# Three issue orders pinned in a two-layer encoder kernel: copies, a weight and two sums

## The chip, the cores and the metric

The kernel runs on one core of a Trainium2 chip. The metric is the time of one execution on the device in microseconds. A core has five engines that each work through their own list of instructions and wait for each other by semaphores: TensorE (PE in the profile: matmuls), ScalarE (ACT), VectorE (DVE), GpSimd (POOL) and SyncE (SP). The last two here mostly issue transfers.

## What is computed

Two layers over 512 tokens of 1024 channels, all in fp32, and a last normalisation:

```python
for l in range(DEPTH):                      # DEPTH = 2
    x = x + 0.5 * swiglu(rms_norm(x, ffn1_norm[l]), ffn1_w_in[l], ffn1_w_out[l])
    x = x + mixer(rms_norm(x, mix_norm[l]), mix_w_in[l], mix_gate_bias[l], na_rpb[l],
                  na_w_out[l], f_w_out[l], mix_w_o[l])
    x = x + 0.5 * swiglu(rms_norm(x, ffn2_norm[l]), ffn2_w_in[l], ffn2_w_out[l])
return rms_norm(x, final_norm)
```

The feed-forward width is 2816. The mixer projects its normalised input to queries, keys, values, Fourier input and two gates, and ends with

```python
y_na = neighbourhood_attention(q, k, v, rpb) @ w_na_out
y_f = fourier_mix(uf) @ w_f_out
g_na = jax.nn.sigmoid(ga + gate_bias[0])
g_f = jax.nn.sigmoid(gf + gate_bias[1])
return (g_na * y_na + g_f * y_f) @ w_o
```

## The kernel before

**Precision.** Every operand of a matmul is split in two parts of a shorter format, high (`hi`, written by ScalarE as a copy) and low (`lo`, what is left, written by VectorE). A product is then three matmuls, high by high, high by low and low by high. Lines 490, 491 and 493 of `late_low` issue them, with the ones that need the weight's low part last in their group.

**Strassen's products.** Most of the large products are done as seven products of half the size, numbered 1 to 7, instead of eight. Their operands are sums and differences of quarters of the activations and of the weights. The activations' sums are made by VectorE and split (`combo`, `parts`; names t1, t2, ... or m1, m2, ...). One half-size product takes two items of weights (two granules), and writes two banks of the accumulation memory (`pair("A")`, `"B"`, `"C"`; `"wA"`, `"wB"`, `"wC"` in the output product). A is used again: products 6, 7 and 4 add into the banks that product 1 began.

**The stream of weights.** `Stream` holds all weight items in order. `next()` gives the item that a product needs now, and first calls `prep`, which prepares the items up to two ahead: it asks for the transfers of items up to eight further (`fetch`, issued on SP's queue at line 147, the added second part on POOL's at line 149), makes a sum of two transferred weights where the item is one (L163), writes the high part `whi` (L190, or L185 with a sign) and the low part `wlo` (L193, or L186). For `whi` and `wlo` there are three buffers each, so an item's high part waits until TensorE is done with the item three before. In the gates and the output product, product 6's raw weight gets a further part added by a transfer on POOL's queue once product 6 is prepared (L195), and is then product 3's.

**Order.** Instructions are traced in program order. A scheduler, which runs at build time with a model of the machine, then chooses each engine's order: among the instructions that it takes to be ready, the one traced first. Two means pin it. Instructions traced in a block `tc.manual_schedule(engines=...)` keep their order on those engines. In a block `tc.issue_after(ins)`, whatever is traced on the engine of `ins` is issued behind `ins`; nothing waits for `ins` to end.

**The plain block** is the first work of the first layer (`stage_ffn`, `if first`). The 256 columns of gate and 256 of up that are left over are computed as a plain product of eight steps over the channels, from four weight items (`ws.items[0]` to `[3]`), into the banks `cl`. In the same place, in a block with pinned order for VectorE and ScalarE, the differences of the activations are made that Strassen's products need (L660, L661, L665, L667, and their parts).

**The gates** (`gate_block`, called twice in each layer's mixer) do the seven products in the order 1, 5, 2, 6, 7, 3, 4. After product 6, `snap(pa)` copies both banks of A with ScalarE (L560), and the gate's tanh follows (L1348); product 7 then adds into the same banks. In the first block of each layer `fourth` follows, which makes the operand of product 4.

**The output product** at the end of the mixer (`stage_mixer`, from L1700) does the same on the gated sum, which is first turned to channels by transposes (L1424, copied out in L1425; `mq`). Products 1, 5 and 2 run first; the operands of product 6 (a6) and product 2 (a2) are made while TensorE does product 1 and 5.

Of the kernel before, what the change touches and what calls it, by code (L numbers as in the profile page):

```python
# [13 lines left out]
AF = mybir.ActivationFunctionType  # L14
ALU = mybir.AluOpType
# [74 lines left out]
def encoder_kernel(  # L90
# [3 lines left out]
    V, S, G, PE = nc.vector, nc.scalar, nc.gpsimd, nc.tensor  # L94
# [15 lines left out]
    def slot(dt=F32, s="k", shape=(4, 256)):  # L110
        return kp.tile([P, *shape], dt, tag="k", name=nm(s), bufs=23)
# [8 lines left out]
    def pair(s="ps"):  # L120
        return [bank(s), bank(s)]
# [188 lines left out]
    ws = Stream()  # L310
# [7 lines left out]
    def split(hi, lo, src, scale=None):  # L318
        if scale is None:
            S.activation(hi, src, AF.Copy)  # L320
            V.tensor_tensor(lo, src, hi.bitcast(F32), ALU.subtract)
            return
        S.activation(hi, src, AF.Copy, scale=scale)
        V.scalar_tensor_tensor(lo, src, scale, hi.bitcast(F32), ALU.mult, ALU.subtract)
# [161 lines left out]
    def late_low(parts, again=False):  # L486


        for ps, lh, ll, rh, _, start, _ in parts:
            PE.matmul(ps, lh, rh, start=start, stop=False, skip_group_check=again)  # L490
            PE.matmul(ps, ll, rh, start=False, stop=False, skip_group_check=again)  # L491
        for ps, lh, _, _, rl, _, stop in parts:
            PE.matmul(ps, lh, rl, start=False, stop=stop, skip_group_check=again)  # L493

    def product(ps, acts, kts, start, stop=True, again=False, hook=None, by_block=False, ahead=AHEAD):

        h, l, off = acts
        n = (len(kts) + 1) // 2  # L500

        def granule(i, w, b):
            res = []
            for k, kt in enumerate(kts[2 * i : 2 * i + 2]):
                c, z = slice(off + b * P, off + (b + 1) * P), slice(k * T, (k + 1) * T)
                res.append((
                    ps[b], h[:, kt, c], l[:, kt, c], w[0][:, z], w[1][:, z], start and i + k == 0,
                    stop and 2 * i + k == len(kts) - 1,
                ))
            return res  # L510

        if by_block:
            w = [ws.next() for _ in range(n)]
            for b in range(2):
                for i in range(n):
                    late_low(granule(i, w[i], b), again)
            return
        for i in range(n):
            w = ws.next(AHEAD if i < n - 1 and ahead else ahead)
            if i < n - 1:  # L520
                late_low(granule(i, w, 0) + granule(i, w, 1), again)
            else:
                late_low(granule(i, w, 0), again)
                late_low(granule(i, w, 1), again)
            if hook and i == 0:
                hook()
# [19 lines left out]
    def combo(dst, in0, in1, op, s):  # L546
        V.tensor_tensor(dst, in0, in1, op)
        return parts(dst, s)

    def parts(src, s):  # L550
        h, l = slot(F32R, s + "h"), slot(F32R, s + "l")
        split(h, l, src)
        return h, l, 0
# [3 lines left out]
    def snap(ps):  # L557
        t = slot(F32, "sn", (2, T))
        for b in range(2):
            S.activation(t[:, b, :], ps[b], AF.Copy)  # L560
        return t

    def less(ps, t):
        for b in range(2):
            res = V.tensor_tensor(t[:, b, :], ps[b], t[:, b, :], ALU.subtract)  # L565
        return res
# [30 lines left out]
    def stage_ffn(norm, nxt, late):  # L597
# [50 lines left out]
        if first:  # L648
            for g in range(2):
                w = ws.next()  # L650
                for kk in range(2):
                    plain(2 * g + kk, w, kk, (0, 1))
            w2 = [ws.next(), ws.next()]
            for js in ((1,), (0,)):
                for g in range(2):
                    for kk in range(2):
                        plain(4 + 2 * g + kk, w2[g], kk, js)
            with tc.manual_schedule(engines={mybir.EngineType.DVE, mybir.EngineType.Activation}):
                b11, b12, b21, b22 = raw[0, 0], raw[0, 1], raw[1, 0], raw[1, 1]
                V.tensor_tensor(b11, b11, b12, ALU.subtract)  # L660
                V.tensor_tensor(b12, b12, b22, ALU.subtract)  # L661
                acts[5] = parts(b11, "t1")
                norm.squares(0, 0)
                norm.squares(1, 0)
                V.tensor_tensor(b22, b22, b11, ALU.add)  # L665
                acts[7] = parts(b12, "t3")
                V.tensor_tensor(b21, b21, b22, ALU.subtract)  # L667
                acts[6] = parts(b22, "t2")
                ws.prep(ws.pos + 3)
                norm.squares(0, 1)  # L670
                norm.squares(1, 1)
                split(*t4, b21)
# [162 lines left out]
        for jb in range(0 if first else 1, NB):  # L835
            f0 = 2 + 4 * jb
            if first and jb == 0:
                with tc.manual_schedule(engines={mybir.EngineType.DVE, mybir.EngineType.Activation}):
                    pa = pair("A")
                    product(pa, acts[1], K4, True)  # L840
                    for j in range(2):
                        t = snap(pcl[j])
# [33 lines left out]
        ps = {}  # L876
# [120 lines left out]
    def stage_mixer(l, norm, nxt):  # L997
# [338 lines left out]
        def gate_block(i, bias, acts, after):  # L1336

            r = norm.r

            def arg(src, which, j):  # L1340
                t = src if src is not None else slot(F32, "ga", (2, T))
                for b in range(2):
                    c = 2 * j + b
                    V.scalar_tensor_tensor(
                        t[:, b, :], pa[b] if src is None else t[:, b, :], r[:, c : c + 1],
                        bias[which][:, i * T : (i + 1) * T], ALU.mult, ALU.add,
                    )
                S.activation(t, t, AF.Tanh, scale=0.5)  # L1348
                return t

            def gated(t, y):
                V.scalar_tensor_tensor(y, t, 1.0, y, ALU.add, ALU.mult)

            done = []

            def both(j):

                if j in done and (i, j) in ns:
                    V.tensor_tensor(fs[i, j], fs[i, j], ns[i, j], ALU.add)
                done.append(j)  # L1360

            def with_f(t, j):
                gated(t, fs[i, j])
                both(j)

            def with_n(t, j):
                if (i, j) in ns:
                    gated(t, ns[i, j])
                    both(j)
                else:  # L1370
                    ga[j] = t

            ga = [None, None]
            for m in ORDER:
                if m == 1:
                    pa = pair("A")
                    product(pa, acts[1], K4, True)
                    s1 = snap(pa)
                elif m == 5:
                    pb = pair("B")  # L1380
                    product(pb, acts[5], K4, True)
                    sb = snap(pb)
                elif m == 6:
                    product(pa, acts[6], K4, False, again=True)
                    with tc.manual_schedule(engines={mybir.EngineType.Activation}):
                        s2 = snap(pa)
                        with_n(arg(s1, 0, 0), 0)
                elif m == 2:
                    pc = pair("C")
                    product(pc, acts[2], K4, True)  # L1390
                    less(pc, s1)
                elif m == 7:
                    product(pa, acts[7], K4, False, again=True)
                    less(pa, sb)
                    with_f(arg(sb, 1, 1), 1)
                elif m == 3:
                    product(pb, acts[3], K4, False, again=True)
                    less(pb, s2)
                    with_n(arg(s2, 0, 1), 1)
                else:  # L1400
                    product(pa, acts[4], K4, False, again=True)
                    with_f(arg(None, 1, 0), 0)
                if m in after:
                    after[m]()
            return ga if (i, 0) not in ns else [fs[i, 0], fs[i, 1]]
# [46 lines left out]
        with tc.manual_schedule(engines={mybir.EngineType.DVE, mybir.EngineType.Activation}):  # L1452
            with tc.manual_schedule(engines={mybir.EngineType.PE}):
# [60 lines left out]
                for s in range(3):  # L1514
                    t = slot(F32R, "vs", (2, T))
# [184 lines left out]
        def fourth():  # L1700
            with behind_weights():
                V.tensor_tensor(t12, B[1, 0][0], t12, ALU.subtract)
                V.tensor_tensor(t12, t12, B[1, 0][1], ALU.add)
                split(hx[0][:, :, 256:512], lx[0][:, :, 256:512], t12)

        ga0 = gate_block(0, bias, acts, {1: third_parts, 6: fourth})

        ga1 = gate_block(1, bias, acts, {5: lambda: to_channels(0, ga0, 1), 2: lambda: to_channels(0, ga0, 0)})
        m00, m01 = mq[0, 0], mq[0, 1]
        a1 = parts(m00, "m1")  # L1710
# [7 lines left out]
        m11 = mq[1, 1]  # L1718
        to_channels(1, ga1, 0)
        m10 = mq[1, 0]  # L1720
        a6 = combo(m00, m00, m11, ALU.add, "m6")
        a2 = parts(m10, "m2")
        pb = pair("wB")
        product(pb, a5, K4, True)
        put(pb, 1, 1, -1)
# [220 lines left out]
```

## Time and profile before

| | us |
|---|---|
| three runs: lowest, median, highest | 1896.66, 1898.59, 1898.66 |
| the profiled execution, as timed | 1897.87 |
| its span, first to last instruction | 1896.1 |
| TensorE busy in it | 1883.8 |
| VectorE busy | 1647.4 |
| ScalarE busy | 1188.6 |
| GpSimd busy | 171.5 |

A row of the order of time has the start in us from the span's start, the time that the instruction (or a run of equal ones, x their number) took, the engine, the line of the kernel, the operation, what it writes `<-` what it reads, their shapes, and in brackets how long the engine had been idle before and what ended that. A row of the list of waits has who waited `<-` for whom, the time in all, how many times, and the longest. In a row of stretches, the busy time of TensorE, its weight loads, VectorE, ScalarE and GpSimd stands with the number of instructions, and then the granted clock, the share of the transfer engines and GB/s.

### The profile page before, as it was taken

How to read it: one execution, taken by the hardware profiler on the slowest of the kernel's cores; microseconds unless marked ns; L12 is line 12 of the kernel's file. 1: busy time of each engine (PE TensorE's matmuls, PEld its weight loads, DVE VectorE, ACT ScalarE, POOL GpSimd, SP SyncE). 2: the span in 40 equal slices, each digit the busy share in tenths (PEclk: the TensorE clock that was granted, in tenths of full speed). 3: DMA queues.
4: the chain of work that ended last, by engine and by line, in shares of the span. 5: the costliest groups of instructions: out<-in, count | busy, mean ns of one | idle time of the engine just before them, and what ended most of it. 6: DMA issues, size and time to landing. Idle time of an engine off the chain costs nothing.

```text
span 1896.1 us, 25080 instructions
## 1 busy us (share of the span) xinstructions
PE 1883.8 (99%) x9150; PEld 1578.6 (83%) x9150; DVE 1647.4 (87%) x2006; ACT 1188.6 (63%) x1700; POOL 171.5 (9%) x210
## 2 busy tenths in 40 slices
PE   9999999999999999999999999999999999999998
PEld 7888888888888888888888888888888888888886
DVE  7877899788989987889998778998889899887899
ACT  6655665668665755566665556666685576556664
POOL 0101011100111010001010100101001101100010
PEclk9999999999999999999999999999999999999999
DMA  9777498932886777649867764988248867766594
GB/s 302 208 201 189 152 244 262 230 102 98 242 219 163 183 191 204 178 151 258 254 193 202 194 174 154 267 267 213 84 137 229 215 169 177 207 177 178 173 278 143
DMA packets 106940, 372.75 MB, mean 197 GB/s; under 512 B 12288, under 2 KB 12416, under 8 KB 106816
## 3 DMA queue, kind: packets, MB, share of 16 engines
q1 hardware_dynamic: 78144, 272.80, 41.7%
q0 software_dynamic: 28528, 98.33, 28.5%
q8 instruction: 72, 1.18, 0.2%
q14 instruction: 52, 0.43, 0.1%
q10 hardware_dynamic: 144, 0.02, 0.0%
HBM read 365.85 MB, written 2.11 MB: 194 GB/s over the span
## 4 chain that ended last, share of the span: by engine, by line
PE 96%; DMA 1%; DVE 1%; issue 1%; SPq 0%; ACT 0%; POOL 0%; DVEq 0%; POOLq 0%; ACTq 0%
PE A L490 10%; PE A L491 10%; PE A L493 10%; PE o L493 7%; PE o L490 7%; PE o L491 7%; PE B L490 5%; PE B L491 5%; PE B L493 5%; PE ps L314 4%; PE ps L315 4%; PE ps L316 3%; PE C L491 2%; PE C L490 2%; PE C L493 2%; PE tr L613 2%
## 5 line engine op out<-in xcount | busy, mean ns | idle before, releaser
L190 ACT ACTIVATE whi<-raw 128x1024 fp32r<-128x1024 f32 (+1 forms) x534 | 551.4, 1037 | 388.5 <-PE A L491 124.2
L193 DVE TENSOR_TENSOR wlo<-raw,whi 128x1024 fp32r<-128x1024 f32 (+1 forms) x534 | 633.3, 1192 | 167.7 <-ACT whi L190 166.4
L149 POOL DMA_DIRECT2D raw<-in_wst_dram x166 | 144.4, 899 | 1369.9 <-DMA raw<-in_wst_dram 927.9
L163 DVE TENSOR_TENSOR raw<-raw,raw 128x1024 f32<-128x1024 f32 (+1 forms) x150 | 177.4, 1190 | 1.2
L490 PE MATMUL A<-whi,xh 128*128 128x512 f32 x400 | 155.7, 389 | 0.0
L491 PE MATMUL A<-whi,xl 128*128 128x512 f32 x400 | 155.7, 389 | 0.0
L493 PE MATMUL A<-wlo,xh 128*128 128x512 f32 x400 | 115.1, 389 | 0.0
L185 ACT ACTIVATE whi<-raw 128x1024 fp32r<-128x1024 f32 (+1 forms) x83 | 85.8, 1037 | 42.2 <-PE o L491 14.0
L186 DVE SCALAR_TENSOR_TENSOR wlo<-raw,whi 128x1024 fp32r<-128x1024 f32 (+1 forms) x83 | 98.0, 1194 | 12.7 <-ACT whi L185 12.7
L695 ACT ACTIVATE th<-sn,rh 128x512 f32<-128x512 f32 x80 | 56.9, 715 | 69.7 <-DVE sn L565 69.7
L560 ACT ACTIVATE sn<-A 128x512 f32<-128x512 f32 x104 | 60.8, 589 | 45.8 <-PE A L493 45.7
L493 PEld LDWEIGHTS A<-wlo,xh 128*128 128x128 f32 x400 | 75.1, 188 | 15.6
L491 PEld LDWEIGHTS A<-whi,xl 128*128 128x128 f32 x400 | 75.1, 188 | 15.4
L490 PEld LDWEIGHTS A<-whi,xh 128*128 128x128 f32 x400 | 75.1, 188 | 15.4
L490 PE MATMUL C<-whi,xh 128*128 128x512 f32 x208 | 81.2, 390 | 0.0
L491 PE MATMUL C<-whi,xl 128*128 128x512 f32 x208 | 81.0, 389 | 0.0
L490 PE MATMUL B<-whi,xh 128*128 128x512 f32 x208 | 81.0, 389 | 0.0
L491 PE MATMUL B<-whi,xl 128*128 128x512 f32 x208 | 81.0, 389 | 0.0
L493 PE MATMUL C<-wlo,xh 128*128 128x512 f32 x208 | 59.8, 389 | 0.0
L493 PE MATMUL B<-wlo,xh 128*128 128x512 f32 x208 | 59.8, 389 | 0.0
L490 PE MATMUL B<-whi,t5h 128*128 128x512 f32 x136 | 54.3, 399 | 0.0
L715 DVE TENSOR_TENSOR at<-at,at 128x1024 f32<-128x1024 f32 (+1 forms) x48 | 53.7, 1127 | 0.0
(448 smaller groups left out, 4786.0 us busy)
## 6 DMA issues: line engine op xcount, KB each, us to landing
raw<-in_wst_dram SPq DMA_DIRECT2D x470, 512.0 KB, 5.4
raw<-in_wst_dram POOLq DMA_DIRECT2D x174, 512.0 KB, 8.1
raw<-in_wst_dram SPq DMA_DIRECT2D x30, 256.0 KB, 4.1
bm<-in_bias_dram SPq DMA_DIRECT2D x16, 384.0 KB, 3.8
vs<-v SPq DMA_DIRECT2D x12, 256.0 KB, 3.8
x<-in_xin_dram SPq DMA_DIRECT2D x4, 512.0 KB, 10.2
raw<-in_wst_dram POOLq DMA_DIRECT2D x8, 256.0 KB, 8.2
dft<-in_dft_dram POOLq DMA_DIRECT2D x8, 256.0 KB, 4.4
```

What stands on the lines that cost most here:

```text
L149: G.dma_start(out=self.t, in_=wst[GRAN_AT[self.plus]][:, 0 : self.n], accum_op=ALU.add)
L163: V.tensor_tensor(self.raw.t, self.raw.t, self.add.t, ALU.add)
L185: S.activation(hi, t, AF.Copy, scale=-1.0)
L186: self.last = V.scalar_tensor_tensor(lo, t, -1.0, hi.bitcast(F32), ALU.mult, ALU.subtract)
L190: S.activation(hi[:, cs], t[:, cs], AF.Copy)
L193: self.last = V.tensor_tensor(lo[:, cs], t[:, cs], hi[:, cs].bitcast(F32), ALU.subtract)
L314: PE.matmul(ps, lh, rh, start=start, stop=False, skip_group_check=again)
L315: PE.matmul(ps, lh, rl, start=False, stop=False, skip_group_check=again)
L490: PE.matmul(ps, lh, rh, start=start, stop=False, skip_group_check=again)
L491: PE.matmul(ps, ll, rh, start=False, stop=False, skip_group_check=again)
L493: PE.matmul(ps, lh, rl, start=False, stop=stop, skip_group_check=again)
L560: S.activation(t[:, b, :], ps[b], AF.Copy)
```

## The change

Three places get an issue order. No instruction is added or taken out.

1. *Plain block.* What VectorE does in the block of differences is issued behind the low part of the fourth weight item, the plain block's last.
2. *Gates.* `snap` keeps its last copy's instruction. Before product 7, the fetch that the coming preparation would ask for is asked for, and the preparation up to product 3's first weight is traced in a block behind the second copy of product 6: on ScalarE, `whi` of that weight is issued after both copies.
3. *Output product.* The sum for product 6 with its parts, the parts for product 2, and the preparation of weights up to product 2's first are put in one block with pinned order for VectorE and ScalarE.

```diff
@@ snap
-            S.activation(t[:, b, :], ps[b], AF.Copy)
+            snapped[0] = S.activation(t[:, b, :], ps[b], AF.Copy)
         return t
+
+    snapped = [None]
@@ stage_ffn, plain block
-            with tc.manual_schedule(engines={mybir.EngineType.DVE, mybir.EngineType.Activation}):
+            with (
+                tc.issue_after(ws.items[3].last.ins),
+                tc.manual_schedule(engines={mybir.EngineType.DVE, mybir.EngineType.Activation}),
+            ):
                 b11, b12, b21, b22 = raw[0, 0], raw[0, 1], raw[1, 0], raw[1, 1]
                 V.tensor_tensor(b11, b11, b12, ALU.subtract)
@@ gate_block
                     with tc.manual_schedule(engines={mybir.EngineType.Activation}):
                         s2 = snap(pa)
+                        copied = snapped[0]
                         with_n(arg(s1, 0, 0), 0)
...
                 elif m == 7:
+                    ws.fetch(ws.pos + 2 + ws.depth)
+                    with tc.issue_after(copied.ins):
+                        ws.prep(ws.pos + 3)
                     product(pa, acts[7], K4, False, again=True)
@@ stage_mixer, output product
-        a6 = combo(m00, m00, m11, ALU.add, "m6")
-        a2 = parts(m10, "m2")
+        with tc.manual_schedule(engines={mybir.EngineType.DVE, mybir.EngineType.Activation}):
+            a6 = combo(m00, m00, m11, ALU.add, "m6")
+            a2 = parts(m10, "m2")
+            ws.prep(ws.pos + 3)
         pb = pair("wB")
         product(pb, a5, K4, True)
```

## The prediction

> **What bounds the kernel.** I read the page first, then the list of who waited for whom on TensorE, then the order of time around each of the three places.
>
> ```profile
> span 1896.1 us, 25080 instructions
> PE 1883.8 (99%) x9150; PEld 1578.6 (83%) x9150; DVE 1647.4 (87%) x2006; ACT 1188.6 (63%) x1700; POOL 171.5 (9%) x210
> PEclk9999999999999999999999999999999999999999
> ...
> PE A L490 <- ACT sn L560: 1.0, 1, 1.0
> PE o L493 <- DVE wlo L193: 0.4, 1, 0.4
> PE cl L493 <- DVE wlo L193: 0.3, 1, 0.3
> ```
>
> TensorE is busy for 1883.8 of 1896.1 us, at full clock in every slice. So no edit here can give more than pauses between matmuls, and an edit costs nothing while it makes no new pause. The change takes no matmul, copy, sum or transfer away and adds none: 9150 matmuls stay. It only says which instruction of ScalarE and VectorE comes first. The list of waits shows two of the places, the gates (A waits for sn) and the plain block (cl waits for wlo); the third is too short for it.
>
> The pace against which I count a pause is that of undisturbed matmuls in the gates of layer 0:
>
> ```profile
> 511.60 0.61 PE L493 MATMUL A<-wlo,t3h 128*128 128x512 f32 x2
> 513.21 0.50 PE L490 MATMUL A<-whi,t3h 128*128 128x512 f32 x1 [0.99 <-ACT sn L560]
> 513.55 0.40 PE L491 MATMUL A<-whi,t3l 128*128 128x512 f32 x1
> 513.78 0.39 PE L490 MATMUL A<-whi,t3h 128*128 128x512 f32 x1
> ...
> 517.42 0.39 PE L490 MATMUL B<-whi,xh 128*128 128x512 f32 x1
> ...
> 509.54 0.60 ACT L560 ACTIVATE sn<-A 128x512 f32<-128x512 f32 x1 [1.20 <-PE A L493]
> 511.62 1.06 ACT L190 ACTIVATE whi<-raw 128x1024 fp32r<-128x1024 f32 x1 [1.48 <-DMA raw<-in_wst_dram]
> 512.58 0.58 ACT L560 ACTIVATE sn<-A 128x512 f32<-128x512 f32 x1
> 513.06 1.05 ACT L1348 ACTIVATE sn<-sn 128x1024 f32<-128x1024 f32 x1
> ```
>
> A product is 24 matmuls. The row at 513.78 is the ninth of product 7 and that at 517.42 the first of product 3, 16 starts later: 3.64/16 = 0.2275 us a matmul.
>
> **Gates, four times (two blocks in each of two layers).** Product 7 adds into the banks of A, so it must wait until ScalarE has copied what product 6 left there. ScalarE served copy of bank 0 (509.54), then the high part of product 3's first weight (511.62), whose transfer was late, then the copy of bank 1 (512.58). Product 7's matmul on bank 1 started at 513.21. From 511.60, its fifth matmul, to 513.78, its ninth, are four starts: 2.18 us where 4 x 0.2275 = 0.91 would do. **The pause is 1.27 us.** With the new edge the second copy no longer stands behind the weight. It can begin when bank 1 is done, six matmuls after bank 0: 509.54 + 1.37 = 510.91, end 511.49. The matmul is due at 511.60 + 2 x 0.2275 = 512.06, so 0.57 us stay in hand and the whole pause goes. Bounds: 0 if something else holds that matmul, 1.27 at most; I take 1.27, since the wait row names this copy alone. The fetch that now stands ahead asks for the same items as the one inside the preparation; no transfer is moved past another, neither on SP's nor on POOL's queue.
>
> [...]
>
> In the other three gate blocks the transfer was in time and the order costs little:
>
> ```profile
> 1453.02 0.48 PE L490 MATMUL A<-whi,t3h 128*128 128x512 f32 x1
> 1453.33 0.40 PE L491 MATMUL A<-whi,t3l 128*128 128x512 f32 x1
> ...
> 1451.40 1.06 ACT L190 ACTIVATE whi<-raw 128x1024 fp32r<-128x1024 f32 x1 [0.31 <-PE A L491]
> ```
>
> 0.31 instead of 0.23 between two starts: 0.08 to 0.09 us in block 0 of layer 1. I take 0.09 there and the same for the second block of each layer, which issues the same order: 0.27. Bounds 0 and 0.27.
>
> What the edge costs: the weight's high part now waits for the copy, and so do all ScalarE instructions behind it. In layer 1 it could start at 1451.40 and will now start a good microsecond later. If the tanh (1.05, row 513.06), and in block 0 the equally large high part of the fourth operand, also go ahead, then in layer 0 it ends at 511.49 + 1.05 + 1.05 + 1.06 = 514.65. Product 3 needs it at 517.42 - 1.27 = 516.15: 1.5 us in hand, so I cost it at nothing. VectorE's low part (1.23) then ends at about 516 to 517 and is due eight matmuls into product 3, at 517.97.
>
> **Plain block, once (first layer).**
>
> ```profile
> 19.02 0.61 PE L493 MATMUL cl<-wlo,xh 128*128 128x512 f32 x2
> ...
> 21.03 0.72 PE L493 MATMUL cl<-wlo,xh 128*128 128x512 f32 x2 [0.27 <-DVE wlo L193]
> 21.59 0.40 PE L490 MATMUL cl<-whi,xh 128*128 128x512 f32 x1
> ...
> 17.50 1.06 ACT L320 ACTIVATE t1h<-xr 128x1024 fp32r<-128x1024 f32 x1 [1.86 <-DVE xr L660]
> 18.46 1.05 ACT L190 ACTIVATE whi<-raw 128x1024 fp32r<-128x1024 f32 x1
> ...
> 16.24 1.22 DVE L660 TENSOR_TENSOR xr<-xr,xr 128x1024 f32<-128x1024 f32 x1
> 17.38 0.75 DVE L324 SCALAR_TENSOR_TENSOR xl<-xt,gn,xh 128x512 fp32r<-128x512 f32 x1
> ...
> 19.75 1.22 DVE L193 TENSOR_TENSOR wlo<-raw,whi 128x1024 fp32r<-128x1024 f32 x1
> ...
> 5.72 1.89 SPq L147 DMA_DIRECT2D raw<-in_wst_dram  x3
> ...
> raw<-in_wst_dram SPq DMA_DIRECT2D x10, 512.0 KB, 9.8
> ```
>
> From 19.02 to 21.59 are eight starts: 2.57 us against 1.82, a pause of 0.75. VectorE did the first difference (16.24) ahead of the last weight's low part (19.75); ScalarE stood idle for 1.86 us for that difference's high part and only then made the weight's. The weight was issued at 5.72 and by the median of that window's transfers landed 9.8 us later, at 15.5. So with the difference behind it, ScalarE can make the high part at 15.6, and VectorE's list moves up by one instruction, 17.38 - 16.24 = 1.14 us: the low part ends at 19.75 - 1.14 + 1.22 = 19.83, due at 19.02 + 6 x 0.2275 = 20.39. The pause goes: 0.75. Bounds: 0 if the landing was as late as 18.4, 0.75 at most. What is queued behind: the difference, its high part and the squares on ScalarE, which that engine's idle time takes up. What is late next are the weights of product 5:
>
> ```profile
> 40.59 1.22 DVE L193 TENSOR_TENSOR wlo<-raw,whi 128x1024 fp32r<-128x1024 f32 x1
> 42.94 0.61 PE L493 MATMUL B<-wlo,t1h 128*128 128x512 f32 x2
> ```
>
> The second of them ends at 41.81 and was read at 42.94; 0.75 earlier leaves 0.38 us. That is cover, though little; if ScalarE comes 1 us later here, 0.6 of the 0.75 is lost again.
>
> **Output product, twice.**
>
> ```profile
> 591.82 0.61 PE L490 MATMUL wC<-whi,m2h 128*128 128x512 f32 x2
> 593.92 1.07 PE L493 MATMUL wC<-wlo,m2h 128*128 128x512 f32 x4
> ...
> 586.61 1.21 DVE L193 TENSOR_TENSOR wlo<-raw,whi 128x1024 fp32r<-128x1024 f32 x1
> 591.15 1.22 DVE L321 TENSOR_TENSOR m2l<-mq,m2h 128x1024 fp32r<-128x1024 f32 x1
> ...
> 1531.59 0.61 PE L490 MATMUL wC<-whi,m2h 128*128 128x512 f32 x2
> 1533.69 1.09 PE L493 MATMUL wC<-wlo,m2h 128*128 128x512 f32 x4
> ```
>
> Eight starts take 2.10 us in both layers, 0.28 more than 1.82: product 2's low operand m2l ends at 592.37, after its product began at 591.82. Pinned ahead of product 2's first weight (wlo at 586.61), m2l moves up by one such instruction, some 1.1 us, to about 591.2; its first reader is due at 592.05. So 0.28 goes in each layer: **0.56**; bounds 0 and 0.56. The weight's low part takes m2l's old place and ends near 592.4, due at 593.6. Its raw buffer is freed up to 4 us later, and the load waiting for it on SP's queue with the ones behind it; those weights are for product 4 and the next feed-forward, products away, so I cost that at nothing.
>
> **Sum.** 1.27 + 0.27 + 0.75 + 0.56 = 2.85 us. The profiled execution took 1897.87 (its span and 1.8 around it), which gives 1895.0. The median of the runs shown is 1898.59, 0.72 above it; as that is what a measurement would be compared with, I forecast 1898.59 - 2.85 = **1895.7 us**, 0.15% less. No change is told from change here beyond 0.2%, or 3.8 us; the three runs lie 2.0 us apart.
>
> **Rivals.**
>
> ```profile
> 505.00:530.00 25.00, 24.00 (x106) 19.55 (x105) 24.16 (x27) 14.44 (x15) 4.28 (x5) 1.00 0.99 251
> 1446.00:1471.00 25.00, 25.00 (x111) 20.56 (x110) 24.93 (x28) 15.35 (x16) 4.18 (x5) 1.00 0.98 243
> ```
>
> *The gates' gain is given back.* VectorE is busy 24.16 of 25 us around the pause. If it is what sets the pace there, TensorE's 1.27 returns as a wait for a weight's low part or for a bank: 1895.74 + 1.27 = 1897.0. Against it: in layer 1 the same list runs at 24.93 of 25 us with TensorE never idle, so VectorE keeps up. Chance 0.12.
>
> *More than forecast.* The schedule is made anew, and other pauses may go with these, above all the one of o for wlo (0.4 in the list, once): 1895.74 - 0.4 and about 0.5 of restarting: 1894.8. For it: the pause is no necessity, it stands once among four feed-forwards. Against it: nothing in the diff touches it. Chance 0.12.
>
> *Slower.* Place: ScalarE's queue in the gates. The copy that now stands ahead waits for TensorE, and product 3's weight stands behind it. It decides from 1.5 us of further delay (above): one more instruction of 1.05 is borne, three are not, 3.15 - 1.5 = 1.65 in each of four gates, 6.6 in all, 1895.7 + 6.6 = 1902.3. For it: where instructions outside the pinned ones go is decided anew, and the late transfer of layer 0 (1.48 of idle before 511.62) shows how one head of the queue holds all. Against it: after the copy only the tanh and one high part are at hand. Chance 0.14. [...]
>
> **How the numbers follow.** Forecast 0.62, its own range 1894.3 to 1897.2. By the runs' scatter a quarter of it would be measured as more than 3.8 us (0.15), with 0.09 of the second rival: faster 0.24. Slower by over 0.2% is 0.10 of the third rival's 0.14. The rest, 0.66, is within 0.2%. The range 1893.4 to 1900.0 takes in the forecast with all lower bounds (nothing gained, 1898.6) and half of the slower case.
>
> **What would show it.** Right: no row of A waiting for sn on TensorE; in the gates both sn copies back to back ahead of whi; cl waiting for wlo gone, L660 after the weight's low part; m2l ahead of wlo, and eight starts of wC in 1.82 us; TensorE's last matmul some 2.8 us earlier. Wrong: a new wait of B for whi or wlo after 516 us or at 38 to 43 us; different orders in the feed-forward blocks; a span that moved by over 4 us.

## The result, and the profile after

| | before | after |
|---|---|---|
| median of 7 runs, us | 1898.14 | 1904.78 |
| lowest and highest | 1896.14, 1900.03 | 1902.6, 1906.26 |
| profiled execution, as timed | 1897.87 | 1904.78 |
| its span | 1896.1 | 1903.0 |

The change makes the kernel slower: the ratio of the times is 1.0036, with an interval of 1.0025 to 1.0048. Forecast was 1895.7 us, with 1900.0 as the upper end of the range. The span moved by 6.9 us, which is more than the 4 us that the prediction names as a sign of being wrong.

The page of the kernel after, its line of busy times:

```profile
PE 1886.8 (99%) x9150; PEld 1580.4 (83%) x9150; DVE 1647.1 (87%) x2006; ACT 1187.5 (62%) x1700; POOL 171.5 (9%) x210
```

These 6.9 us are not more work: VectorE and ScalarE are as busy as before, and TensorE has the same 9150 matmuls. Its list of waits for the kernel after (who waited, for whom, us in all, times, longest):

```profile
PE tr L395 <- DVE x L1766: 4.9, 2, 2.5
...
PE wA L491 <- DVE m4l L321: 0.8, 1, 0.8
```

The waits that the change aimed at (A for sn, cl for the weight's low part) are gone. Two new ones are there: the transposes of the next norm wait for the updates of x, once in each layer, and product 4 of the output product waits once for its operand m4l. Both lie at the end of the output product, about a hundred matmuls behind the pinned place.

**Where the pauses went.** The gates of layer 0 in the order of time, kernel after:

```profile
508.48 0.60 ACT L560 ACTIVATE sn<-A 128x512 f32<-128x512 f32 x1 [1.20 <-PE A L493]
509.84 0.60 ACT L560 ACTIVATE sn<-A 128x512 f32<-128x512 f32 x1 [0.76 <-PE A L493]
510.34 1.05 ACT L1353 ACTIVATE sn<-sn 128x1024 f32<-128x1024 f32 x1
511.28 1.05 ACT L320 ACTIVATE xh<-t 128x1024 fp32r<-128x1024 f32 x1
512.23 2.00 ACT L190 ACTIVATE whi<-raw 128x1024 fp32r<-128x1024 f32 x2
...
515.17 0.39 PE L490 MATMUL B<-whi,xh 128*128 128x512 f32 x1
```

The second copy starts 1.36 us after the first, when its bank is done; the tanh and the fourth operand slip in ahead of the weight, and the high parts of both of product 3's weights (the row x2) are still ready by 514.23, 0.94 us before product 3 begins. Product 3 starts at 515.17 where it stood at 517.42. The plain block and the low part m2l did as forecast too, in the same kernel:

```profile
18.34 0.61 PE L493 MATMUL cl<-wlo,xh 128*128 128x512 f32 x2
...
18.61 1.21 DVE L193 TENSOR_TENSOR wlo<-raw,whi 128x1024 fp32r<-128x1024 f32 x1
19.75 1.21 DVE L665 TENSOR_TENSOR xr<-xr,xr 128x1024 f32<-128x1024 f32 x1
...
21.06 0.61 PE L493 MATMUL cl<-wlo,xh 128*128 128x512 f32 x2
...
589.56 0.39 PE L490 MATMUL wC<-whi,m2h 128*128 128x512 f32 x1
...
591.37 1.07 PE L493 MATMUL wC<-wlo,m2h 128*128 128x512 f32 x4
```

The last weight's low part is now ahead of the first difference, and from 18.34 to 21.06 cl has twelve starts in 2.72 us, the undisturbed pace. From 589.56 to 591.37 are eight starts of product 2 in 1.81 us; the 0.28 is gone.

**Where the time was lost.** Three matmuls place it: the first of product 7 in layer 0 and the first of the next feed-forward in both layers. Kernel before:

```profile
602.98 0.39 PE L490 MATMUL wA<-whi,m7h 128*128 128x512 f32 x1
...
621.44 0.39 PE L490 MATMUL A<-whi,xh 128*128 128x512 f32 x1
...
1561.11 0.39 PE L490 MATMUL A<-whi,xh 128*128 128x512 f32 x1
```

and kernel after:

```profile
600.82 0.39 PE L490 MATMUL wA<-whi,m7h 128*128 128x512 f32 x1
...
625.39 0.40 PE L490 MATMUL A<-whi,xh 128*128 128x512 f32 x1
...
1568.01 0.39 PE L490 MATMUL A<-whi,xh 128*128 128x512 f32 x1
```

At product 7 of layer 0 the changed kernel is 2.16 us ahead (0.9 of it by luck: a pause of `o` at 316 us in the profile before is absent in this one); at the feed-forward it is 3.95 behind: 6.11 us lost within some 20 us. The same matmul of layer 1 is 6.90 behind, another 2.95 lost in the 940 us between, nearly all of it again at the end of the output product, as shown below.

**Why: VectorE's list.** In the output product of layer 0, kernel before (the first two rows of L193 are the low parts of product 6's two weights):

```profile
593.49 1.21 DVE L1726 TENSOR_TENSOR mq<-mq,mq 128x1024 f32<-128x1024 f32 x1
...
595.75 1.22 DVE L193 TENSOR_TENSOR wlo<-raw,whi 128x1024 fp32r<-128x1024 f32 x1
596.89 1.21 DVE L321 TENSOR_TENSOR m7l<-mq,m7h 128x1024 fp32r<-128x1024 f32 x1
598.03 1.22 DVE L321 TENSOR_TENSOR m3l<-mq,m3h 128x1024 fp32r<-128x1024 f32 x1
599.16 1.22 DVE L193 TENSOR_TENSOR wlo<-raw,whi 128x1024 fp32r<-128x1024 f32 x1
...
607.76 1.23 DVE L193 TENSOR_TENSOR wlo<-raw,whi 128x1024 fp32r<-128x1024 f32 x1 [1.02 <-ACT whi L190]
```

The same stretch, kernel after (the difference for product 7 is now L1737, the update of x L1766; of the row x2 at 597.51 the first is product 6's):

```profile
585.49 1.21 DVE L1737 TENSOR_TENSOR mq<-mq,mq 128x1024 f32<-128x1024 f32 x1
...
592.37 1.21 DVE L321 TENSOR_TENSOR m7l<-mq,m7h 128x1024 fp32r<-128x1024 f32 x1
593.50 1.21 DVE L321 TENSOR_TENSOR m3l<-mq,m3h 128x1024 fp32r<-128x1024 f32 x1
...
595.77 1.21 DVE L193 TENSOR_TENSOR wlo<-raw,whi 128x1024 fp32r<-128x1024 f32 x1
...
597.51 2.35 DVE L193 TENSOR_TENSOR wlo<-raw,whi 128x1024 fp32r<-128x1024 f32 x2
...
610.10 1.23 DVE L193 TENSOR_TENSOR wlo<-raw,whi 128x1024 fp32r<-128x1024 f32 x1 [4.02 <-ACT whi L190]
...
612.38 1.28 DVE L1766 SCALAR_TENSOR_TENSOR x<-wA,x 128x512 f32<-128x512 f32 x2
613.59 1.22 DVE L321 TENSOR_TENSOR m4l<-mq,m4h 128x1024 fp32r<-128x1024 f32 x1
...
619.50 0.68 DVE L1766 SCALAR_TENSOR_TENSOR x<-wB,x 128x512 f32<-128x512 f32 x1
```

The difference for product 7 moved from 593.49 to 585.49, and m7l and m3l, which stood behind the low part of product 6's first weight, now stand ahead of it. That low part runs at the same time as before (595.77, before 595.75) although TensorE has come 2 us ahead. The two low parts of product 6 are also closer: they start 3.41 us apart before (599.16 - 595.75), 1.74 after.

What hangs on these two is a transfer each: L195 on POOL's queue adds the further part to the raw weight and makes it product 3's. POOL's issues and ScalarE's high part of product 3's second weight, kernel before:

```profile
597.97 0.87 POOL L195 DMA_DIRECT2D raw<-in_wst_dram  x1 [26.40 <-DVE wlo L193]
600.92 0.86 POOL L195 DMA_DIRECT2D raw<-in_wst_dram  x1 [2.07 <-ACT whi L190]
...
606.67 1.06 ACT L190 ACTIVATE whi<-raw 128x1024 fp32r<-128x1024 f32 x1 [1.31 <-DMA raw<-in_wst_dram]
```

and kernel after:

```profile
598.22 1.76 POOL L195 DMA_DIRECT2D raw<-in_wst_dram  x2 [27.14 <-ACT whi L190]
...
609.01 2.01 ACT L190 ACTIVATE whi<-raw 128x1024 fp32r<-128x1024 f32 x2 [3.58 <-DMA raw<-in_wst_dram]
```

Before, the two transfers left 2.95 us apart and the second was used 5.75 us after its issue. After, they leave back to back, the second at 599.01 by the record of its issue (0.79 behind the first), and its data is used 10.0 us later, at 609.01. The second left 1.9 us earlier in the profile's time and landed 2.3 us later, while TensorE was 2.2 us ahead. Now the row at 610.10 reads itself: VectorE stands 4.02 us at the head of its list for that weight's high part, and behind it stand the updates of x and m4l. TensorE has work meanwhile and then meets what is late: m4l, and the x of 619.50, the last one that the transposes need. TensorE's rows there, kernel after:

```profile
613.61 0.49 PE L490 MATMUL wA<-whi,m4h 128*128 128x512 f32 x1
614.87 0.50 PE L491 MATMUL wA<-whi,m4l 128*128 128x512 f32 x1 [0.77 <-DVE m4l L321]
...
617.50 0.27 PE L395 MATMUL tr<-ident,x 128*128 128x128 f32 x1
620.23 0.98 PE L395 MATMUL tr<-ident,x 128*128 128x128 f32 x7 [2.47 <-DVE x L1766]
...
1564.43 0.98 PE L395 MATMUL tr<-ident,x 128*128 128x128 f32 x7 [2.44 <-DVE x L1766]
```

By starts, the wait for m4l is 1.26 - 0.23 = 1.03 us and that of the transposes 2.73 - 0.11 = 2.62. A third loss is not a wait. Stretches of the kernel after (columns as explained above; the granted clock is the third number from the end), right behind the transposes' wait, layer 0 and layer 1:

```profile
621.50:625.40 3.90, 3.90 (x12) 3.02 (x11) 3.61 (x4) 2.54 (x6) 0.56 (x1) 0.56 0.57 222
1565.20:1569.00 3.80, 3.80 (x19) 3.15 (x18) 3.52 (x4) 3.77 (x9) 0.00 (x0) 1.00 0.85 281
```

In layer 0 the granted clock is 0.56 on average over these 3.9 us, and 0.50 in the part from 621.6 to 624.9: matmuls started 0.43 us apart there instead of 0.23, and the ten starts from 621.52 to 625.39 took 3.87 us instead of 2.28, or 1.6 us more. In layer 1, after an equal wait, it stayed at 1.00, and the loss there is hardly more than the wait. So layer 0's 6.11 is 2.62 + 1.03 + 1.6 and, for the rest, short pauses (the largest 0.28); of layer 1's 2.95 the transposes' wait is 2.60.

### The profile page after: what moved, and what is told of

It is laid out like the page before. It is cut to its first block, busy times and chain, and to the rows that moved or that the text cites. A ratio compares the mean times of both kernels' runs of the same rounds, so it can differ in the third digit from the quotient of the medians.

```text
span 1903.0 us, 25071 instructions
## 1 busy us (share of the span) xinstructions
PE 1886.8 (99%) x9150; PEld 1580.4 (83%) x9150; DVE 1647.1 (87%) x2006; ACT 1187.5 (62%) x1700; POOL 171.5 (9%) x210
## 4 chain that ended last, share of the span: by engine, by line
PE 94%; DVE 3%; DMA 1%; ACT 1%; issue 1%; POOL 0%; DVEq 0%; ACTq 0%
PE A L490 10%; PE A L491 10%; PE A L493 10%; PE o L491 7%; PE o L490 7%; PE o L493 7%; PE B L490 5%; PE B L491 5%; PE B L493 5%; PE ps L314 4%; PE ps L315 4%; PE ps L316 4%; PE C L491 2%; PE C L490 2%; PE C L493 2%; PE tr L615 2%
## 5 line engine op out<-in xcount | busy, mean ns | idle before, releaser
L193 DVE TENSOR_TENSOR wlo<-raw,whi 128x1024 fp32r<-128x1024 f32 (+1 forms) x534 | 632.3, 1192 | 175.3 <-ACT whi L190 174.1
```

The costliest lines, as they stand in the source:

```text
L193: self.last = V.tensor_tensor(lo[:, cs], t[:, cs], hi[:, cs].bitcast(F32), ALU.subtract)
```

## The experiments

The theory, called the held list, has the loss come from the output product's block alone, by the way just read. The first rival, pace, has TensorE run early into transfers that can't come sooner, because parts 1 and 2 gained 2 us; then any gain ahead of the output product would be lost there. The ratios below are to the kernel before, run on the same chip.

**parts12**: plain block and gates as in the change, the output product as before.

```diff
-        with tc.manual_schedule(engines={mybir.EngineType.DVE, mybir.EngineType.Activation}):
-            a6 = combo(m00, m00, m11, ALU.add, "m6")
-            a2 = parts(m10, "m2")
-            ws.prep(ws.pos + 3)
+        a6 = combo(m00, m00, m11, ALU.add, "m6")
+        a2 = parts(m10, "m2")
```

> The plain block and the gates as in the change, the output product as before. Theory 'held list' (the loss comes from the output product's pinned block alone): no pause of over 0.5 us in either output product, the gates' 1.27 us pause gone, 2 to 3.5 us faster than before. Rival 'pace' (TensorE, some 2 us earlier through the first two parts, runs into transfers that land when they land): pauses of 1 to 3 us in the first layer's output product, no faster than before by 1 us.

Measured: median 1896.37 against 1898.49 us, ratio 0.9993 (0.9985 to 1.0002), span 1894.3. In its list of TensorE's waits one row is left beside the one for the ones of the first microseconds:

```profile
PE o L491 <- DVE c4l L321: 0.3, 1, 0.3
```

TensorE comes early here too (the transposes of layer 0 start at 615.12, before at 617.66), and no wait of the output product reaches the list: pace falls. The expected gain of 2 to 3.5 us is not there: it is 1.3 us by the ratio, at the edge of what the runs tell from none.

**part3**: the pinned block alone, on the kernel before.

```diff
+        with tc.manual_schedule(engines={mybir.EngineType.DVE, mybir.EngineType.Activation}):
+            a6 = combo(m00, m00, m11, ALU.add, "m6")
+            a2 = parts(m10, "m2")
+            ws.prep(ws.pos + 3)
-        a6 = combo(m00, m00, m11, ALU.add, "m6")
-        a2 = parts(m10, "m2")
```

> Only the output product's pinned block. Held list: in both layers the transposes wait about 2.6 us for the update of x, the second added transfer of product 6's weight lands 8 to 10 us after its issue, and the kernel is 5 to 9 us slower than before. Pace: without the first two parts TensorE is not early, so no such waits, and 0.3 to 0.6 us faster than before.

Measured: median 1906.73, ratio 1.0046 (1.0034 to 1.0059). The waits:

```profile
PE tr L395 <- DVE x L1757: 4.9, 2, 2.4
...
PE wA L491 <- DVE m4l L321: 0.8, 1, 0.8
```

The block alone makes the whole loss, with the same two waits. It is the cause; what in it remains to be separated. Against pace this run says less than was meant: its profile, too, has TensorE 1.7 us ahead of the profile before at 580 us, without the first two parts. It is parts12, 2.6 us ahead there and with no loss, that refutes pace.

**after_first6**: the whole change, and product 6's first weight prepared ahead of product 7's difference and the parts behind it.

```diff
         put(pb, 1, 1, -1)
+        ws.prep(ws.pos + 3)
         V.tensor_tensor(m01, m01, m11, ALU.subtract)
         a7 = parts(m01, "m7")
         a3 = parts(m11, "m3")
```

> The whole change, and product 6's first weight is prepared ahead of product 7's difference and of the operands of products 7 and 3. Held list: the first added transfer leaves some 2 us earlier against TensorE, the two leave 2.5 us or more apart, the second lands within 7 us, and the 2.6 us waits of the transposes go: 2 to 4 us faster than before. Pace: as slow as the change, 1904 to 1906 us.

Measured: median 1896.94, ratio 0.9994 (0.9985 to 1.0003), span 1894.4. The 2.6 us waits of the transposes and the one for m4l are gone, in exchange for two small ones of product 7 for an update of x:

```profile
PE wA L490 <- DVE x L1767: 0.5, 2, 0.3
```

One line of order gives back 7.8 us by the medians (1904.78 - 1896.94). Two numbers of the expectation were missed. The gain over the kernel before is 1.1 us by the ratio and not told from none, where 2 to 4 were expected. And in layer 0 the transfers left only 1.55 us apart, and the second took 8.4; POOL's rows there:

```profile
593.91 0.87 POOL L195 DMA_DIRECT2D raw<-in_wst_dram  x1 [23.25 <-DVE wlo L193]
595.46 0.86 POOL L195 DMA_DIRECT2D raw<-in_wst_dram  x1 [0.69 <-DVE wlo L193]
```

But the second left at 595.46, 3.5 us earlier than in the change, and so it landed at 603.88, in time. So two transfers close together are not enough for the loss; the second must also be needed soon.

**after_no_add**: the change with the second of the two adding transfers left out in the output product.

```diff
-                    add(d, a, then=b.key if dma else None)
+                    add(d, a, then=b.key if dma and not (name('a') == 'wa' and g == 1) else None)
```

> The whole change, but in the output product nothing is added to the raw weight of product 6's second half, so product 3 uses another weight there. VectorE's and ScalarE's lists are those of the change. If the late landing is the cause: the 4 us and 3 us for which VectorE stands idle ahead of product 3's second weight go, the transposes' wait falls under 0.6 us, and the kernel is 2 to 4 us faster than before. If the order of VectorE's list itself is too long there: the transposes still wait over 1.5 us and it stays above 1901 us.

Measured: median 1897.79, ratio 0.9997 (0.9988 to 1.0007). VectorE at the place where it stood 4.02 us, and TensorE's transposes:

```profile
606.97 1.23 DVE L193 TENSOR_TENSOR wlo<-raw,whi 128x1024 fp32r<-128x1024 f32 x1 [0.33 <-ACT whi L190]
...
617.11 0.98 PE L395 MATMUL tr<-ident,x 128*128 128x128 f32 x7 [0.67 <-DVE x L1766]
```

The order of the change is all there, but for the one transfer. By starts the transposes' wait is 0.83 us in layer 0 and 0.19 in layer 1, where it was 2.6 in both; the wait for m4l and the drop of the clock are gone. So the late landing carries most of the loss, and the order by itself the 0.8 that the expectation had put below 0.6. The expected gain of 2 to 4 us over the kernel before is not there either: 0.6 us by the ratio, not told from none.

**held6**: parts 1 and 2 with nothing pinned in the output product, but product 6's first weight issued behind m3l on VectorE.

```diff
-        a3 = parts(m11, "m3")
+        a3h, a3l = slot(F32R, "m3h"), slot(F32R, "m3l")
+        S.activation(a3h, m11, AF.Copy)
+        held = V.tensor_tensor(a3l, m11, a3h.bitcast(F32), ALU.subtract)
+        a3 = (a3h, a3l, 0)
+        with tc.issue_after(held.ins):
+            ws.prep(ws.pos + 3)
```

> Parts 1 and 2 and no pinned block in the output product; instead product 6's first weight is issued on VectorE behind the low parts of the operands of products 7 and 3. If it is that place in the list which loses the time: the transposes wait over 1.5 us for the update of x in both layers and the kernel is 4 to 10 us slower than parts 1 and 2 alone (1900 to 1907 us). Rival 'late product 2' (the loss comes from what the pin itself delays, product 2's weight and the buffer and loads behind it): product 2's weight is early here, so no wait over 0.5 us and 1896 to 1897 us.

Measured: median 1909.67 against 1898.11, ratio 1.0055 (1.0042 to 1.0069). The waits:

```profile
PE tr L395 <- DVE x L1769: 4.9, 2, 2.5
PE wA L493 <- DVE wlo L193: 2.0, 2, 1.0
```

With product 2's weight left where it was and only product 6's held, the transposes' wait comes back, so a delay of product 2's weight is not needed for the loss. It came out slower than expected, for two reasons that the profile shows: product 6 itself waits some 1.15 us by starts for the low part in each layer, and the clock falls behind the transposes' wait in both layers:

```profile
621.50:625.40 3.90, 3.90 (x15) 3.23 (x14) 3.62 (x4) 3.11 (x7) 0.00 (x0) 0.56 0.94 298
1568.20:1572.00 3.80, 3.80 (x14) 3.01 (x13) 3.52 (x4) 2.41 (x5) 0.00 (x0) 0.70 0.71 240
```

**after_first6_m3**: after_first6, with product 3's parts moved behind the update of x that product 7 waited for.

```diff
-        a3 = parts(m11, "m3")
...
                 put(pc, 0, 0, 1, (1,))
+                a3 = parts(m11, "m3")
                 product(pa, a7, K4, False, again=True)
```

> The whole change, product 6's first weight ahead as in after_first6, and product 3's operand split behind both updates of x from product 6. The two waits of 0.41 us of product 7 for those updates should go (under 0.15 us each); all else as in after_first6. 0.4 to 0.8 us faster than after_first6, 2 to 4 us faster than before. If the updates are not what that wait hangs on, it stays.

Measured: median 1896.41 against 1898.11, ratio 0.9991 (0.9982 to 1.0000). Product 7's two pauses went from 0.41 to 0.11 us. In layer 0 the transposes now wait 0.5 us by starts for an update of x, so not all else is as in after_first6, and the two are not told apart by their times. It is 8.4 us faster than the change by the medians, and at the edge of being faster than the kernel before (1.7 us by the ratio, where 2 to 4 were expected).

**part2** and **part1**: the gates' order alone, and the plain block's alone, one execution each; the edits are those of the change.

> The gates' order alone. Both copies stand ahead of the weight in all four blocks; the 1.27 us pause at about 513 us goes, and the 0.08 us in the other three; from product 7's fifth matmul to its ninth 0.91 us instead of 2.18. The plain block keeps its pause of 0.75 us between 19 and 22 us. Product 3 has no wait for its weight.

> The plain block's order alone. The eight starts from about 19.0 us take 1.82 us instead of 2.57; the weights of product 5 (38 to 43 us) cause no new pause; the gates keep their 1.27 us pause unless the added transfer lands earlier.

With the gates' order alone (span 1896.3) no gate block pauses; a wait for c4l late in the last feed-forward took 1.46 us by starts. With the plain block's alone (span 1894.0) the pause of cl is gone, and the gates, whose order is that of before, paused only 0.29 us. So the 1.27 us of the profile before belong to that execution, in which one transfer landed late (7.8 us after its issue at 503.70, where the same one took 5.8 in the profile after), and not to each. The plain block's 0.75 us are no constant either: part2 was expected to keep them, but in it, and in part3, whose plain block is also as before, the same eight starts take 2.01 us, a pause of 0.19. TensorE came to that place 0.8 to 1.0 us later in these two.

The two adding transfers, in the kernels whose order there differs, as issue of the second behind the first, and then issue to landing of the second, us:

| | layer 0 | layer 1 |
|---|---|---|
| before | 2.95, 5.6 | 3.65, 5.5 |
| parts12 | 2.94, 5.6 | 3.65, 5.8 |
| after_first6 | 1.55, 8.4 | 2.27, 6.0 |
| after | 0.79, 9.9 | 1.50, 8.1 |
| part3 | 0.79, 9.1 | 1.50, 8.4 |
| held6 | 0.79, 9.1 | 1.50, 8.3 |
| after_first6_m3 | 1.56, 8.5 | 2.27, 6.1 |

## Why the prediction was wrong

- **Gates.** The mechanism was right in each step: copies back to back, 1.36 us apart (forecast 1.37), the tanh and a high part ahead of the weight, the weight ready in time. The size was that of one execution: 1.27 where part1's profile had 0.29 to lose and part3's, with the same order, 0.17.
- **Plain block.** Right: the low part ahead of the first difference, and the pause gone. In this execution the first four matmuls of cl started 0.59, 0.43 and 0.38 us apart (0.33, 0.27 and 0.23 in the profile before), after a start 0.14 us later, so that TensorE was 0.7 us behind from there on, which took most of the 0.75 back. The start of that block varies, and with it what there is to gain (0.75, or 0.19 in part2 and part3).
- **Output product, m2l.** Right: eight starts in 1.81 us, 0.28 gained in layer 0 as forecast.
- **The sum of the gains.** Parts 1 and 2 together were forecast at 1.27 + 0.27 + 0.75 = 2.29 us; parts12 gives 1.3 by its ratio (0.0007 x 1898.49), and its interval reaches from a gain of 2.8 to a loss of 0.4. Nothing there is refuted.
- **The step that failed** is the cost of the third part, which the output product's last sentence puts at nothing: "those weights are for product 4 and the next feed-forward, products away, so I cost that at nothing". The loads named there were not shown to cost anything; in held6, where product 2's weight is not delayed, the loss comes all the same. What failed is what the sentence leaves out: I followed m2l and the one weight that it passed, and let every other instruction of VectorE stand where it stood. But the scheduler chooses all of the rest anew. With product 2's first weight pinned behind the two sums, the difference for product 7 came ahead of it all (585.49), and its low part and product 3's, which are traced ahead of product 6's weights, followed (592.37 and 593.50). So product 6's first low part came no earlier although TensorE was 2 us ahead, and the second followed it closely. Their two adding transfers left 0.79 us apart instead of 2.95, and the second took 9.9 us instead of 5.6. Product 3's second weight came late by it, and VectorE's list, standing 4.02 us for that weight, passed the delay on to m4l and to the updates of x. That cost 6.1 us in layer 0 and 2.95 in layer 1, against 0.56 gained.
- **What could have been seen.** The kernel before already has ScalarE idle for 1.31 us for the second of these transfers (row 606.67): ScalarE has no slack for a later landing there. The same trace also shows what a close pair costs, in the gates, where L195 issues such pairs too: 1.30 us apart, at 503.70 and 505.00 and at 1444.60 and 1445.90, the second transfers took 9.6 and 8.6 us, and the first of layer 0, at 7.8, is the late one behind the 1.27 us pause. In the output product, 2.95 and 3.65 us apart, they took 5.6 and 5.5. So 3 to 4 us for bringing two such transfers together (8.6 - 5.5 and 9.6 - 5.6, an estimate) could have been read off ahead of the run.
- **The slower rival** had the right kind of mechanism, a head of an engine's list that hands its wait on (here VectorE's 4.02 us ahead of the row at 610.10), and 1902.3 us for it. Its place was wrong: ScalarE in the gates, where three more instructions would have been needed, and not VectorE in the output product. The gain-given-back rival named VectorE as the engine that sets the pace, but in the gates too. The pause of `o`, on which the rival of a larger gain stood, was absent in the profile after, but it comes and goes (below).

Not tried, and so open: what slows the second adding transfer. It is issued on POOL's queue like the first, and in layer 0 a load on SP's queue is issued behind it, 0.9 us behind in the change (at 599.88), 1.2 us in the kernel before (at 602.13). That load, too, took longer in the change (9.2 us, 5.8 before), and from the first issue to the last landing of the three it is 10.9 us in the change and 10.0 before. No run takes the load away, so whether it has a part in this is not shown. Open too are two pauses of `o` that come and go between executions whatever the edit: one at 316 us (0.6 us by starts at its first matmul in the profile before, absent in the one after), and the one for c4l at 1876 us, between 0.2 and 1.46 where it shows.

## What to carry to other kernels

A pinned order can move more than what is pinned (here the difference for product 7, from 593.49 to 585.49 us), so write down the new list of the whole engine, and look at which instructions that release a transfer came to stand behind others. Look also for an engine that idles for a transfer ahead of a high or low part, even where TensorE's list of waits shows nothing: ScalarE, idle for 1.31 us for one before, stood 3.58 us when it landed 2.3 us later. What a closer issue does to the landing can be looked up where the same kernel already issues such pairs (8.6 and 9.6 us in the gates). And a pause of one profiled execution that rests on a transfer's landing is worth its mean over executions, not its size in one; a second profile shows how far it varies (here 1.27, 0.29 and 0.17 us).

## What the runs showed of the hardware

Of two adding transfers of 512 KB on POOL's queue in the output product, issued 2.9 us apart or more, the second took 5.5 to 5.8 us (kernel before, parts12). Issued 2.3 us apart it took 6.0 to 6.1 (layer 1 of after_first6 and after_first6_m3), 1.5 us apart 8.1 to 8.5 (layer 0 of these two, layer 1 of after, part3 and held6), and 0.8 us apart 9.1 to 9.9 (layer 0 of after, part3 and held6): in the kernel after it left 1.9 us earlier than before and landed 2.3 us later. The distance alone did not set it: in the gates, 1.3 us apart, the second took between 7.0 us (kernel after, issued at 503.94) and 9.6 us (kernel before, at 505.00).

TensorE's granted clock fell behind the transposes' wait (idle time 2.4 to 2.5 us in its rows, 2.6 us by starts) in four of the six places where that wait stands. In layer 0 of the kernel after it was 0.50 for 3.4 us, from 621.55 to 624.97. In held6 it was 0.56 on average over 3.9 us in layer 0 and 0.70 over 3.8 us in layer 1 (the rows of stretches above), and in layer 0 of part3 matmuls started 0.43 us apart from 621.38 on. In layer 1 of the kernel after it stayed at 1.00; part3 ran there at the same pace, 8.58 us from VectorE's last update of x before the transposes (1563.76) to ScalarE's first copy of A (1572.34), where the kernel after has 8.60. The size of the pause at m4l ahead of the wait does not tell these apart: it is 0.3 us in layer 1 of held6, where the clock fell, and of part3, where it did not. What tells them apart was not shown: no run was made to test it. By these runs a wait of 2.6 us is not safe: the clock fell behind four of the six.
